# Moving every SBUF tile of a hybrid attention encoder to a multiple of 512 bytes

## The chip, the cores and the metric

The kernel runs on one core of one Trainium2 chip. The metric is the device time of one execution in microseconds (us). The time before is 1574.03 us, the median of three runs (1571.99 to 1578.36).

Five engines work side by side on one core: TensorE (PE in the profile; its weight loads are PEld), VectorE (DVE), ScalarE (ACT), GpSimd (POOL) and SyncE (SP), which here issues the transfers. They share the on-chip memory SBUF, in which a tile is a stretch of bytes at the same address in each of 128 partitions.

## What is computed

One layer of an encoder on 1024 positions of 1024 channels, all in float32, with a conditioning vector c that gives six vectors of shifts, scales and gates:

```
ada = silu(c) @ w_ada + b_ada          # shift1, scale1, gate1, shift2, scale2, gate2
h = rmsnorm(x, g_mix) * (1 + scale1) + shift1
qa, ka, va, qb, kb, vb, ga, gb = split(h @ w_in)
oa = mixture_of_dilations(qa, ka, va)             # three dilated windows, 8 heads of 64
ob = neighbourhood_attention_2d(qb, kb, vb)       # 16 x 64 grid, 8 heads of 64
merged = sigmoid(ga) * (oa @ w_branch_dil) + sigmoid(gb) * (ob @ w_branch_na)
x = x + gate1 * (merged @ w_out)
h2 = rmsnorm(x, g_ffn) * (1 + scale2) + shift2
u = depthwise_conv3(h2 @ w_up)                    # 2 x 2816 channels
x = x + gate2 * ((gelu(u_gate) * u_val) @ w_down)
return rmsnorm(x, g_final)
```

## The kernel before

**Arithmetic.** TensorE multiplies in a float32 form of less precision, so each operand is split into a high and a low part (`split`, line 54: ScalarE copies, then GpSimd or VectorE subtracts) and each product is three matmuls: high by high, high by low, low by high. `product` (line 72) does so for the plain products, on lines 77 to 79; `products` (line 800) does it on lines 822 to 824 for the up and down projections, which are run as a seven-product block scheme. Nearly all of these matmuls load 128x128 weights and stream 512 columns.

**Stages in order of time** (us from the start of the span):

- to about 150: the modulation vectors and the two value projections. The matmuls of `v_products` have h as weights and the tiles a0, a1, b1, b2 as moving operand.
- to about 700: per head pair, the query and key projections (`qk_tiles`), the two attentions, and the gate projections (`gate_tile`) between them. `q_half`, `k_half` and `gate_tile` use weights from the tiles whi and wlo; for the second attention the query product is line 378, with 256 columns each.
- to about 803: the two branch projections with weights from whi and wlo, moving operands o0 and o1.
- to about 886: the output projection (`out_tile`), again with whi and wlo, moving operands mhi and mlo.
- to about 1320: the up projection, 22 blocks of seven products of twelve matmuls. Products "11" and "12" take their weights from whi and wlo, the others from wsh, wsl and big.
- to the end: the down projection, twelve jobs of seven products of nine matmuls, with the same division of the weights, and the last norm.

A planner orders the instructions of each engine, except in stretches that are put under `manual_schedule`. It also makes a tile wait for the last user of the bytes that it takes over (`reuse_waits="tile"`).

**Where tiles lie.** Pools are stacked in SBUF from the low end (left) or, with `side="right"`, from the high end. At address 0 lies a scratch area for transfers that GpSimd issues, 16384 bytes before the change, then four built-in constants of 32 bytes each. So the pool `const` begins at 16512, and everything on the left stands on what lies below it. On the right the stack begins at 229344, which is 32 bytes short of a multiple of 512. Worked out from the sizes in the code, the tiles start at:

| tiles | bytes past a multiple of 512 | side |
|---|---|---|
| idt, sm | 128 | left |
| cs, ones, ada, am1, am2 (32 to 192 bytes each) | 96, 128, 160, 352, 384 | left |
| wraw, whi, wlo (pool `w`) | 416 | left |
| rs (32 bytes, two buffers) | 416, 448 | left |
| all big tiles after pool `w`: t0, a0, a1, b1, b2, qs, ks, kl, vv, P, th, tl, o0, o1, g, wc, big, wsh, wsl, B11 to T4 of the down stage | 480 | left |
| vraw, mt (pool `early`, above the 32 bytes of sig) | 0 | left |
| h, x, gs, mhi, mlo, x2, T1, T2, T3 | 480 | right |

In the down projection the left stack ends exactly where the right one begins (147424).

Lines that the change touches: 41 to 50 (the constants), 93 (rs in `rstd_of`), 256 (sig), 1225 (release of the pools) and 1323 (size of the scratch area).

Of the kernel before, what the change touches and what calls it, by code (L numbers as in the profile page):

```python
# [9 lines left out]
FT = mybir.dt.float32  # L10
# [8 lines left out]
KT = 8  # L19
# [9 lines left out]
def hybrid_encoder(tc, xT, c, w_ada, small, w_in, w_v, p1_bias, p23_bias, na_bias, ln2_mult, ident, w_br, w_out,  # L29
                   w_up, w_down, out):  # L30
    nc = tc.nc
    act, dve, pool, pe, sp = nc.scalar, nc.vector, nc.gpsimd, nc.tensor, nc.sync

    const = tc.alloc_tile_pool(name="const", bufs=1)
    wpool = tc.alloc_tile_pool(name="w", bufs=2)
    dram = tc.alloc_tile_pool(name="scr", bufs=1, space=DRAM)

    def f(ap):
        return ap.bitcast(FT)

    idt = const.tile([128, 128], FT, name="idt")
    sp.dma_start(idt, ident)
    sm = const.tile([128, 248], FT, name="sm")
    cs = const.tile([128, KT], FT, name="cs")
    sp.dma_start(cs, c)
    ones = const.tile([128, 1], FT, name="ones")
    dve.memset(ones, 1.0)
    ada = const.tile([128, 48], FT, name="ada")
    am1 = const.tile([128, KT], FT, name="am1")
    am2 = const.tile([128, KT], FT, name="am2")  # L50
    b_ada, g_mix, g_ffn, g_fin = sm[:, 0:48], sm[:, 48:56], sm[:, 56:64], sm[:, 64:72]
    conv = sm[:, 72:248].rearrange("p (j m) -> p j m", j=4)

# [36 lines left out]
                      stop=last and t == n - 1, skip_group_check=True)  # L90

    def rstd_of(pcol, n):
        r = wpool.tile([128, KT], FT, name="rs", bufs=2)
        dve.tensor_scalar(r[:, :n], pcol[:, :n], 1.0 / D, EPS, OP.mult, OP.add)
        act.activation(r[:, :n], r[:, :n], AF.Sqrt)
        dve.reciprocal(r[:, :n], r[:, :n])
        return r
# [24 lines left out]
    early = tc.alloc_tile_pool(name="early", bufs=1, reuse_waits="tile")  # L122
    ps = tc.alloc_tile_pool(name="ps0", bufs=1, space=PSUM, reuse_waits="tile")
# [129 lines left out]
        for j, t0 in ((0, 0), (8, 240)):  # L253
            sp.dma_start(va_b[j, 0:64, cc].rearrange("(r p) n -> r p n", r=4), v4[:, t0:t0 + 16])

    sig = early.tile([128, KT], FT, name="sig")
    act.activation(sig, cs, AF.Sigmoid)
    dve.tensor_tensor(cs, cs, sig, OP.mult)
    pas = {}
    with tc.manual_schedule(engines={e.engine for e in (sp, act, dve, pool, pe)}):  # L260
# [15 lines left out]
        pcol = norm_sums(accs)  # L276
        acc = ada_rows(rows[0], range(3))
        r = rstd_of(pcol, 4)
        warm(3)
        pb = bcast(r, ps, "pc")  # L280
# [22 lines left out]
        rows = {4: ada_load(4, "t0"), 5: ada_load(5, None)}  # L303
        pcol = norm_sums(accs)
        r = rstd_of(pcol, 4)
        for kp in range(2):
            v_split(raws[kp], vw[1], kp)
# [407 lines left out]
    ps = tc.alloc_tile_pool(name="ps", bufs=1, space=PSUM, reuse_waits="tile")  # L715
    mxpool = tc.alloc_tile_pool(name="mx", bufs=1, side="right", reuse_waits="tile")
# [24 lines left out]
    with tc.tile_pool(name="gate", bufs=1, reuse_waits="tile") as work:  # L741
# [3 lines left out]
        for m in range(KT):  # L745
# [3 lines left out]
            for hf in range(2):  # L749
                sg = []  # L750
                for br in range(2):
# [3 lines left out]
                    p = ps.tile([128, 512], FT, name="pj", bufs=6)  # L755
# [96 lines left out]
    keep = tc.alloc_tile_pool(name="keep", bufs=1, reuse_waits="tile")  # L852
# [128 lines left out]
    add_sums(pcol, sqa, True, False)  # L981
    add_sums(pcol, sq, False, True)
    bc = bcast(rstd_of(pcol, 4), ps, "pbc")
    for k in range(KT):
        dve.tensor_tensor(m1[k], m1[k], bc, OP.mult)
# [23 lines left out]
    with tc.tile_pool(name="up", bufs=2, reuse_waits="tile") as work:  # L1009
# [96 lines left out]
        for t in range(FF):  # L1106
# [8 lines left out]
            for j in gens[t] if t < 2 else up_products(t, sts[t]):  # L1115
# [7 lines left out]
                if t == FF - 1 and j == 3:  # L1123
                    oppool2.release()
                    work2 = tc.alloc_tile_pool(name="down2", bufs=1, side="right", reuse_waits="tile")
# [12 lines left out]
    work1 = {n: tc.alloc_tile_pool(name=n, bufs=1, reuse_waits="tile") for n in ("wsh", "wsl", "B21", "B22", "T4")}  # L1138
# [46 lines left out]
    with tc.manual_schedule(engines={dve.engine}):  # L1185
        for hf, cs in ((0, slice(0, 512)), (1, slice(0, 256)), (1, slice(256, 512))):
            n = cs.stop - cs.start
            late = []
            for m in range(KT):
                if hf == 0 and m + 2 < KT:  # L1190
                    end_w[m + 2] = end_weights(m + 2)
                p = ps.tile([128, 512], FT, name="pj", bufs=6)[:, :n]
# [21 lines left out]
        hf, cs, bc = before  # L1214
# [7 lines left out]
                pool.tensor_tensor(yy, xx, bc, OP.mult)  # L1222
        for m in (0,2,4,6):
            (act if m == 2 else sp).dma_start(out[m:m + 2, :, halves[hf]][:, :, cs].rearrange("t p s -> p t s"), y[m])
    for p in (work2, mxpool, *list(work1.values())[::-1], keep, ps, dram, wpool, const):
        p.release()


# [105 lines left out]
```

## Time and profile before

| | us |
|---|---|
| median of the runs shown | 1574.03 |
| the profiled execution, whole time | 1569.62 |
| its span, first to last instruction | 1567.6 |
| matmuls in the span | 7582 |

The profile is a record of one execution. A group of instructions has its line in the code, engine, tiles (output, then inputs), count, and busy time with the mean of one, or the shortest, median and longest in nanoseconds (ns). Matmuls overlap each other, so the duration of one (389 ns) is longer than the distance from one start to the next; distances are read from the starts in the timeline. Digits are left out of the names of tiles in some views: b1 and b2 are b.

### The profile page before, as it was taken

How to read it: one execution, taken by the hardware profiler on the slowest of the kernel's cores; microseconds unless marked ns; L12 is line 12 of the kernel's file. 1: busy time of each engine (PE TensorE's matmuls, PEld its weight loads, DVE VectorE, ACT ScalarE, POOL GpSimd, SP SyncE). 2: the span in 40 equal slices, each digit the busy share in tenths (PEclk: the TensorE clock that was granted, in tenths of full speed). 3: DMA queues.
4: the chain of work that ended last, by engine and by line, in shares of the span. 5: the costliest groups of instructions: out<-in, count | busy, mean ns of one | idle time of the engine just before them, and what ended most of it. 6: DMA issues, size and time to landing. Idle time of an engine off the chain costs nothing.

```text
span 1567.6 us, 21162 instructions
## 1 busy us (share of the span) xinstructions
PE 1505.0 (96%) x7582; PEld 1266.6 (81%) x7582; DVE 1030.4 (66%) x1873; ACT 777.7 (50%) x1419; POOL 748.4 (48%) x475
## 2 busy tenths in 40 slices
PE   7898999999999999999999989999999999999998
PEld 7687788888878998888778767888888887778787
DVE  7694356576757655525534898677777776877765
ACT  3420566665756666643344444444444446575542
POOL 2310423333214444311146859766677665778621
PEclk8999999999999999999999989999999999999999
DMA  9577632324234565545544212222222223623313
GB/s 378 191 289 268 169 84 89 100 77 114 74 92 133 162 155 134 182 149 183 182 144 148 95 54 94 95 83 88 86 81 81 82 74 135 208 88 126 109 55 108
DMA packets 110000, 205.20 MB, mean 131 GB/s; under 512 B 40356, under 2 KB 55588, under 8 KB 109860
## 3 DMA queue, kind: packets, MB, share of 16 engines
q1 hardware_dynamic: 109624, 203.59, 40.5%
q8 instruction: 60, 0.98, 0.3%
q14 instruction: 44, 0.36, 0.1%
q10 hardware_dynamic: 272, 0.26, 0.1%
HBM read 158.73 MB, written 42.47 MB: 128 GB/s over the span
## 4 chain that ended last, share of the span: by engine, by line
PE 63%; DVE 12%; DMA 9%; POOL 6%; ACT 4%; issue 4%; SPq 1%; DVEq 0%; ACTq 0%; POOLq 0%
PE pj L822 8%; PE pj L823 8%; PE pj L824 8%; PE pj L79 8%; PE pj L77 8%; PE pj L78 8%; DMA wraw<-w_down 3%; DMA g<-gs 2%; DVE mt L151 2%; PE pj L378 2%; PE O L672 2%; POOL wlo L56 2%; POOL wsl L56 2%; DVE big L1017 1%; PE T L660 1%
## 5 line engine op out<-in xcount | busy, mean ns | idle before, releaser
L56 POOL TENSOR_TENSOR wlo<-wraw,whi 128x1024 fp32r<-128x1024 f32 (+1 forms) x77 | 179.4, 2331 | 268.6 <-ACT whi L55 262.3
L77 PE MATMUL pj<-h,whi 128*128 128x512 f32 x448 | 179.7, 401 | 1.8 <-DVE qs L369 1.8
L79 PE MATMUL pj<-h,wlo 128*128 128x512 f32 x448 | 179.9, 402 | 1.3 <-POOL wlo L56 1.3
L78 PE MATMUL pj<-h,whi 128*128 128x512 f32 x448 | 179.3, 400 | 0.0
L1017 DVE SCALAR_TENSOR_TENSOR big<-pj,sm,big 128x512 f32<-128x512 f32 (+2 forms) x252 | 128.4, 565 | 33.1 <-ACT big L1011 33.1
L56 POOL TENSOR_TENSOR wsl<-big,wsh 128x1024 fp32r<-128x1024 f32 (+1 forms) x45 | 109.8, 2442 | 56.9 <-ACT wsh L55 55.7
L1011 ACT ACTIVATE big<-pj,sm 128x512 f32<-128x512 f32 x84 | 63.1, 776 | 123.6 <-DVE pj L840 55.6
L55 ACT ACTIVATE whi<-wraw 128x1024 fp32r<-128x1024 f32 (+1 forms) x79 | 80.7, 1021 | 84.3 <-PE pj L78 27.5
L79 PEld LDWEIGHTS pj<-h,wlo 128*128 128x128 f32 x448 | 85.1, 190 | 16.5 <-POOL wlo L56 1.8
L77 PEld LDWEIGHTS pj<-h,whi 128*128 128x128 f32 x448 | 85.2, 190 | 16.2 <-issue 2.2
L78 PEld LDWEIGHTS pj<-h,whi 128*128 128x128 f32 x448 | 85.1, 190 | 14.6
L449 POOL TENSOR_TENSOR vv<-vv 96x256 fp32r<-96x256 f32 (+2 forms) x32 | 41.1, 1294 | 105.2 <-ACT vv L448 101.8
L498 ACT ACTIVATE P<-P,st 128x256 f32<-128x256 f32 x128 | 64.3, 503 | 51.1 <-DVE st L497 50.8
L385 POOL TENSOR_SCALAR qb<-qs 128x256 fp32r<-128x256 f32 x32 | 26.4, 849 | 122.0 <-PE S L544 57.9
L497 DVE CUSTOM_DVE_ANT_0 P<-S,bias 128x256 f32<-128x256 f32 x128 | 52.4, 420 | 43.4 <-PE S L544 24.7
L650 POOL TENSOR_SCALAR P<-P,stb 128x288 f32<-128x288 f32 (+1 forms) x32 | 40.0, 1249 | 65.6 <-DVE stb L647 58.7
L55 ACT ACTIVATE wsh<-big 128x1024 fp32r<-128x1024 f32 (+1 forms) x45 | 44.9, 1001 | 43.2 <-POOL big L787 21.5
L1044 DVE TENSOR_TENSOR big<-big 128x1024 f32<-128x1024 f32 x22 | 49.7, 2259 | 23.6 <-ACT big L1043 23.6
L56 POOL TENSOR_TENSOR wsl<-wraw,wsh 128x768 fp32r<-128x768 f32 (+1 forms) x23 | 54.5, 2371 | 12.8 <-ACT wsh L55 12.8
L503 DVE TENSOR_TENSOR tl<-T,th 128x512 fp32r<-128x512 f32 x64 | 43.7, 688 | 25.5 <-ACT th L502 25.0
L795 DVE TENSOR_TENSOR wraw<-wraw,big 128x384 f32<-128x384 f32 (+1 forms) x23 | 35.3, 1537 | 34.7 <-POOL big L787 26.5
L79 PE MATMUL pj<-mhi,wlo 128*128 128x512 f32 x128 | 50.7, 396 | 1.8 <-POOL wlo L56 1.8
(366 smaller groups left out, 4785.1 us busy)
## 6 DMA issues: line engine op xcount, KB each, us to landing
wraw<-w_in SPq DMA_DIRECT2D x32, 512.0 KB, 4.4
t<-w_ada SPq DMA_DIRECT2D x24, 512.0 KB, 7.8
big<-w_up SPq DMA_DIRECT2D x22, 512.0 KB, 5.5
wraw<-w_up SPq DMA_DIRECT2D x22, 512.0 KB, 3.5
as<-big SPq DMA_DIRECT2D x22, 512.0 KB, 2.8
big<-as SPq DMA_DIRECT2D x22, 512.0 KB, 6.0
wraw<-w_down SPq DMA_DIRECT2D x24, 384.0 KB, 3.6
x<-w_ada SPq DMA_DIRECT2D x16, 512.0 KB, 8.9
```

Source lines behind the costliest of these rows:

```text
L55: act.activation(hi, raw, AF.Copy)
L56: lo_eng.tensor_tensor(lo, raw, f(hi), OP.subtract)
L77: pe.matmul(psum, whi[:, k0 + k], mhi, start=k == 0, stop=False)
L78: pe.matmul(psum, whi[:, k0 + k], mlo, start=False, stop=False)
L79: pe.matmul(psum, wlo[:, k0 + k], mhi, start=False, stop=k == n - 1)
L497: dve.tensor_tensor_reduce(pp, d, bias, -1.0, BIG, OP.add, OP.min, mi)
L498: act.activation(pp, pp, AF.Exp, bias=mi, scale=-1.0, accum_out=li)
L822: pe.matmul(psum, whi[:, k], bhi, start=j < 4 and k == 0, stop=False, skip_group_check=True)
L823: pe.matmul(psum, whi[:, k], blo, start=False, stop=False, skip_group_check=True)
L824: pe.matmul(psum, wlo[:, k], bhi, start=False, stop=k == n - 1, skip_group_check=True)
L1011: act.activation(y[:, halves[hf]], src, AF.Identity, bias=conv[:, 3, t:t + 1], scale=conv[:, 1, t:t + 1])
L1017: dve.scalar_tensor_tensor(y[:, dst], src, wt, y[:, dst], OP.mult, OP.add)
```

## The change

The constants that are written during the kernel (cs, ones, sig, am1, am2) become slices of one tile `cols` of 384 bytes, sm is padded to 1024 bytes, rs to 256 bytes in each of two buffers. `ada` goes to a pool of its own at the right end and takes 480 bytes there. The scratch area shrinks from 16384 to 8192 bytes.

By the same arithmetic as above: 8192 + 128 + 384 + 512 + 1024 = 10240, so pool `w` begins at 20 x 512, its end is 35328 = 69 x 512, and the right stack begins at 229344 - 480 = 228864 = 447 x 512. All big tiles start at multiples of 512. Tiles of pool `w` go down by 8096 bytes, later ones on the left by 7648, vraw and mt by 7680, and those on the right by 480. Between the two stacks of the down stage 7168 bytes stay free. No instruction is added or removed.

```diff
+    cpool = tc.alloc_tile_pool(name="consts", bufs=1, side="right")
+    ada = cpool.tile([128, 120], FT, name="ada")[:, :48]
+    cols = const.tile([128, 96], FT, name="cols")
+    cs, ones, sig = cols[:, 0:8], cols[:, 8:9], cols[:, 16:24]
+    am1, am2 = cols[:, 24:32], cols[:, 32:40]
     idt = const.tile([128, 128], FT, name="idt")
     sp.dma_start(idt, ident)
-    sm = const.tile([128, 248], FT, name="sm")
-    cs = const.tile([128, KT], FT, name="cs")
+    sm = const.tile([128, 256], FT, name="sm")[:, :248]
     sp.dma_start(cs, c)
-    ones = const.tile([128, 1], FT, name="ones")
     dve.memset(ones, 1.0)
-    ada = const.tile([128, 48], FT, name="ada")
-    am1 = const.tile([128, KT], FT, name="am1")
-    am2 = const.tile([128, KT], FT, name="am2")
...
-        r = wpool.tile([128, KT], FT, name="rs", bufs=2)
+        r = wpool.tile([128, 64], FT, name="rs", bufs=2)
...
-    sig = early.tile([128, KT], FT, name="sig")
...
-    for p in (work2, mxpool, *list(work1.values())[::-1], keep, ps, dram, wpool, const):
+    for p in (work2, mxpool, *list(work1.values())[::-1], keep, ps, dram, wpool, cpool, const):
...
-    nc = bacc.Bacc("TRN2", target_bir_lowering=False, num_devices=1)
+    nc = bacc.Bacc("TRN2", target_bir_lowering=False, num_devices=1, dynamic_dma_scratch_size=8192)
```

## The prediction

> **What bounds the kernel now.** I read the head of the page first, then the chain that ended last, then the table by stages.
>
> ```profile
> PE 1505.0 (96%) x7582; PEld 1266.6 (81%) x7582; DVE 1030.4 (66%) x1873; ACT 777.7 (50%) x1419; POOL 748.4 (48%) x475
> ...
> q1 hardware_dynamic: 109624, 203.59, 40.5%
> ...
> PE 63%; DVE 12%; DMA 9%; POOL 6%; ACT 4%; issue 4%; SPq 1%; DVEq 0%; ACTq 0%; POOLq 0%
> ```
>
> ```profile
> core 0: us, PE busy (x) PEld busy (x) DVE busy (x) ACT busy (x) POOL busy (x), PEclk, DMA share, GB/s
> ...
> 150.00:400.00 250.00, 241.84 (x1387) 208.33 (x1386) 150.22 (x433) 146.68 (x349) 89.03 (x65) 0.99 0.38 105
> 400.00:700.00 300.00, 294.56 (x1818) 262.63 (x1818) 174.50 (x450) 183.33 (x407) 109.87 (x79) 0.99 0.49 134
> 700.00:803.00 103.00, 97.30 (x411) 77.59 (x410) 58.84 (x69) 40.93 (x64) 21.16 (x9) 0.98 0.55 181
> 803.00:886.00 83.00, 82.70 (x376) 68.07 (x375) 37.23 (x41) 37.85 (x53) 53.99 (x29) 1.00 0.44 146
> 886.00:1320.00 434.00, 423.84 (x1849) 347.43 (x1848) 322.56 (x442) 196.07 (x251) 304.35 (x163) 0.99 0.25 84
> ```
>
> TensorE has an instruction in hand for 94 to nearly 100% of these stages, at a granted clock of 0.98 to 1.00. All waits together leave it idle for 1567.6 - 1505.0 = 63 us. So a change of addresses, which removes no instruction, can act in three ways only: an engine takes another time for the same instruction, a transfer takes another time, or a wait or the order changes. For each I look for tiles that lie differently already, since pool `early` (mt, vraw) stands at a multiple of 512 while all others are 416 or 480 past one.
>
> **The change part by part: ScalarE, GpSimd, VectorE, weight loads.** From the views by line, with operations of one shape on tiles of both kinds (shortest, median and longest in ns):
>
> ```profile
> L55 ACT ACTIVATE b<-wraw x4: 613/614/614, 62.0 to 63.6; 128x512 fp32r<-128x512 f32 x4
> L55 ACT ACTIVATE b<-vraw x4: 638/642/643, 66.0 to 67.6; 128x512 fp32r<-128x512 f32 x4
> ```
>
> ```profile
> L56 POOL TENSOR_TENSOR b<-vraw,b x4: 1275/1293/1302, 67.7 to 71.4; 128x512 fp32r<-128x512 f32 x4
> ...
> L56 POOL TENSOR_TENSOR b<-wraw,b x4: 1273/1282/1283, 62.7 to 66.4; 128x512 fp32r<-128x512 f32 x4
> ```
>
> ```profile
> L183 DVE TENSOR_TENSOR mt<-mt x12: 684/692/693, 6.5 to 59.4; 128x512 f32<-128x512 f32 x12
> ```
>
> ```profile
> L759 DVE TENSOR_TENSOR g<-g x16: 691/692/1982, 707.0 to 796.7; 128x512 f32<-128x512 f32 x16
> ```
>
> ```profile
> L140 PEld LDWEIGHTS st<-ones,mt x96: 185/192/339, 18.8 to 146.9; 128*128 128x128 f32 x96
> ...
> L140 PEld LDWEIGHTS st<-cs,t x16: 187/192/193, 46.2 to 48.0; 128*128 128x128 f32 x16
> ```
>
> Reading from vraw at offset 0 instead of wraw at 416 costs ScalarE 28 ns more and GpSimd 11 ns more; an add with all three operands at 0 takes the same 692 ns as with all at 480; a weight load from 0 takes the same 192 ns as from 480. I cost these engines at **nothing**. Bounds: 28 ns more on some 250 splits, about as many as line 55 has, is 7 us of ScalarE work, of which 4% (its share of the chain) would count, so 0 to +0.3 us.
>
> **TensorE.** Here two offsets can be told apart. The timeline of one up block has three products in a row, weights from whi and wlo (416) in the first, from wsh and wsl (480) in the second; the third ends the second:
>
> ```profile
> 1003.39 0.39 PE L822 MATMUL pj<-B21hi,whi 128*128 128x512 f32 x1
> ...
> 1006.14 0.39 PE L822 MATMUL pj<-T1hi,wsh 128*128 128x512 f32 x1
> ...
> 1008.86 0.39 PE L822 MATMUL pj<-T3hi,wsh 128*128 128x512 f32 x1
> ```
>
> Twelve matmuls take 2.75 us with the weights of pool `w` and 2.72 us with the others: 229.2 against 226.7 ns, 2.5 ns apart. The groups of lines show it elsewhere, with matmuls of the same shape and no idle time before them:
>
> ```profile
> L78 PE MATMUL pj<-mlo,whi 128*128 128x512 f32 x21 | 8.3, 394 | 0.0
> L77 PE MATMUL pj<-mhi,whi 128*128 128x512 f32 x21 | 8.2, 392 | 0.0
> L79 PE MATMUL pj<-mhi,wlo 128*128 128x512 f32 x21 | 8.2, 388 | 0.0
> ```
>
> ```profile
> L823 PE MATMUL pj<-B11lo,whi 128*128 128x512 f32 x4 | 1.6, 394 | 0.0
> ...
> L823 PE MATMUL pj<-T1lo,wsh 128*128 128x512 f32 x4 | 1.6, 390 | 0.0
> ```
>
> The mean of 394, 392 and 388 is 391.3, which is 2.3 above the 389 of most groups of the up stage. What sets the tiles of pool `w` apart by their address is that their weights lie 64 bytes off the phase of the moving operand (416 against 480), where wsh, wsl, big and h as weights lie in phase with theirs. After the change all are in phase, at 0. That wlo shows no surplus of its own speaks against a plain rule of offsets; I take the triple as the unit, since its three matmuls push each other.
>
> How many: by the loops, 448 x 3 = 1344 in the query, key and gate products, 384 in the branches, 384 in the output projection, 22 x 24 = 528 in the up and 12 x 18 = 216 in the down projection: 2856 matmuls by 2.5 ns is **7.1 us of TensorE time**. Between 63% (its share of the chain) and 98% (its busy share in these stages) of it reaches the end; I take 80%, so **-5.7 us**. When TensorE is quicker there, the next in line are the splits on GpSimd (6% of the chain), which is why not all is kept. Bounds of the phase effect: from -7 us, when all is kept, to nothing.
>
> For the rest of a matmul's cost I can only ask whether the start of the moving operand counts. In the second attention, the keys of grid column 0 start at 480 past a multiple of 512 (32 past one of 64), and those of column 3 are 160 bytes on, at 128 (a multiple of 64 and of 128). Both stream 288 columns:
>
> ```profile
> 568.63 0.29 PE L639 MATMUL S<-ks,qs 128*128 128x288 f32 x1
> ...
> 569.16 0.28 PE L672 MATMUL O<-th,vv 96*128 96x256 f32 x1
> ```
>
> ```profile
> 628.78 0.30 PE L639 MATMUL S<-ks,qs 128*128 128x288 f32 x1
> ...
> 629.31 0.49 PE L660 MATMUL T<-idt,P 128*96 128x128 f32 x3
> ```
>
> Four matmuls take 0.53 us in both. So a better aligned start alone buys nothing that these rows show. The Trainium skill's page "SBUF — State Buffer" (section "Specifications (TRN2)") gives cachelines of 16 bytes as what an access pays for; since every tile before starts at a multiple of 32, by that rule nothing at all would change. The equal 0.53 us agrees, the 2.5 ns of pool `w` doesn't.
>
> **Transfers.** The issues view has transfers out of and into both kinds of tile:
>
> ```profile
> t<-w_ada SPq DMA_DIRECT2D x24, 512.0 KB, 7.8
> ...
> wraw<-w_up SPq DMA_DIRECT2D x22, 512.0 KB, 3.5
> ...
> gs<-gs SPq DMA_DIRECT2D x32, 256.0 KB, 2.6
> ...
> vraw<-w_v SPq DMA_DIRECT2D x4, 512.0 KB, 6.3
> vas<-mt SPq DMA_DIRECT2D x8, 256.0 KB, 8.3
> ```
>
> Into vraw (offset 0) 512 KB take 6.3 us and into t (480) 7.8 us, both in the crowded first stage; out of mt (0) half as much takes 8.3 us, out of gs (480) 2.6 us in a quieter one. The signs disagree, so I take **0**, and keep the bound for a rival. All issues are SP's and ACT's, none GpSimd's, so the smaller scratch area costs nothing.
>
> **Waits and order.** A left tile now lies 7168 bytes lower against a right one, which changes who waits for whom in three places. The right-hand mhi no longer lies over u1 of the attention; the transfer that last read it and the first write of mhi are far apart. The third buffer of wsh no longer lies over mhi, but all buffers of wsl do still reach over it or already did, and mhi's last reader is done before wsh is first written. Tiles th and tl lie over less of x, which the value projections of the stage before have done with.
>
> ```profile
> 690.60 2.59 DMA ob<-u
> ```
>
> ```profile
> L79 PE MATMUL pj<-mhi,wlo x128: 388/388/628, 789.3 to 884.5; 128*128 128x512 f32 x128
> L55 ACT ACTIVATE mhi<-g x16: 612/615/629, 708.6 to 798.8; 128x512 fp32r<-128x512 f32 x16
> ```
>
> ```profile
> L55 ACT ACTIVATE wsh<-big x45: 830/1061/1064, 886.5 to 1485.2; 128x1024 fp32r<-128x1024 f32 x33, 128x768 fp32r<-128x768 f32 x12
> ```
>
> Nothing there is late now, so **0**. That cols is one tile could make a write of am1 wait for TensorE's readers of cs and ones; VectorE already waits there for the sums that these readers make. The chain in order of time has one such sum:
>
> ```profile
> 18.77 1.07 PE st L140 x8
> ```
>
> If the cover failed, such a wait would come four times: 4 x 1.07 = +4 us.
>
> **Sum.** 0 - 5.7 + 0 + 0. The profiled execution took 1569.62 us and would take 1563.9. It lies below all three runs shown, so I set the sum against their median: 1574.0 - 5.7 = **1568.3 us**. A measurement of this kernel tells 0.5% from no change, 7.9 us: the bounds are 1566.1 and 1581.9.
>
> **Rivals.**
> 1. *The change does nothing for time*: the 2.5 ns belong to something else about pool `w` (its place in memory, or its buffers being written beside). For it: wlo at 416 shows no surplus. 1574.0.
> 2. *The fixed part of a matmul shrinks.* From 226.7 ns for 512 columns and 132.5 ns for 288, a column costs 0.4205 ns and 11.4 ns don't depend on the columns. If misalignment is their cause, 5196 matmuls of 512 columns by 11.4 ns by 80% is 47 us: 1527, or 1550 if half goes. Against it: the equal 0.53 us. The Trainium skill ("TensorE: Matmul & The Clock Gate", section "Back-to-back issue gap") has N/2.4 + 2.5 ns, an estimated 215.8 for 512 columns, 10.9 below this trace, which would put the time at about 1529.
> 3. *Transfers get shorter.* A transfer of 512 KB holds each of 16 engines for 0.405 x 1567.6 x 0.524 / 203.59 = 1.63 us of its 3.5. If one part in nine of that goes, it is 0.11 x 0.47 of the chain's 141 us of DMA, 7.3 us: with the forecast 1561. The Trainium skill ("DMA: Bandwidth & Descriptors", section "How a descriptor splits into AXI transactions") says that a descriptor which doesn't start at a multiple of 256 bytes fetches bytes it doesn't use, one transaction more than eight for 2048 bytes. The rows above don't bear it out.
> 4. *Slower: offset 0 is worse than 480 for the stream of matmuls*, as 416 is. No row has both operands at 0. By the same 2.5 ns on the 5196 - 2856 that are at 480 now and none gained on the rest: 5.9 us; at 5 ns on all 5196, by 80%, 21 us: 1580 to 1595, middle 1586. It decides from 1.9 ns on all.
> 5. *The planner puts another order*, since tiles wait for others: -10 to +15 us, in the attention stages, which aren't under a hand-written order.
>
> **How the numbers follow.** Forecast 0.36 (1562 to 1574; a third of it below 1566.1), rival 1 0.20, rival 2 0.10, rival 3 0.08, rival 4 0.14, rival 5 0.12 (faster 0.04, same 0.02, slower 0.06). Faster: 0.12 + 0.10 + 0.08 + 0.04 = 0.34; same: 0.24 + 0.20 + 0.02 = 0.46; slower: 0.14 + 0.06 = 0.20. The range leaves out most of rival 2 below 1553 and the upper half of rival 4 above 1586.
>
> **What would show it.** Right: twelve matmuls with whi and wlo take 2.72 us, as those with wsh; splits, adds and landings unchanged. Rival 2: twelve take under 2.70 us everywhere. Rival 4: over 2.75 everywhere. Rival 5: an engine's instructions in another sequence in the attention stages. The forecast is wrong if the 2.75 us stays, or if 2.72 moves at all.

## The result, and the profile after

The changed kernel took 1561.43 us (median of four runs, 1559.17 to 1565.12) beside 1573.75 us for the kernel before on the same chip: a ratio of 0.992, with a 95% interval of 0.9891 to 0.9948. That is 12.3 us less, where 5.7 us less had been forecast; measured again in e5 below it was 0.9935 (0.9912 to 0.9957). The profiled execution has a span of 1559.6 us and took 1561.49 us in all.

The head of the page after, the rows that answer to those of before:

```profile
PE 1498.4 (96%) x7582; PEld 1264.8 (81%) x7582; DVE 1031.4 (66%) x1873; ACT 778.1 (50%) x1419; POOL 747.2 (48%) x475
...
q1 hardware_dynamic: 109624, 203.59, 40.0%
...
PE 65%; DVE 12%; DMA 8%; POOL 6%; issue 4%; ACT 4%; SPq 1%; DVEq 0%; ACTq 0%; POOLq 0%
```

TensorE is busy for 6.6 us less (1505.0 to 1498.4), the other engines for the same time within 2 us. The transfers move the same 203.59 MB and hold their engines for 40.0% of a shorter span instead of 40.5%. So two things have become shorter: matmuls and transfers.

**The matmuls.** The timeline of an up block after the change, first matmul of each of the three products (line 822 of before is line 821 here):

```profile
996.88 0.39 PE L821 MATMUL pj<-B21hi,whi 128*128 128x512 f32 x1
...
999.60 0.39 PE L821 MATMUL pj<-T1hi,wsh 128*128 128x512 f32 x1
...
1002.32 0.39 PE L821 MATMUL pj<-T3hi,wsh 128*128 128x512 f32 x1
```

Twelve matmuls now take 2.72 us with the weights whi and wlo, as they do with wsh; before it was 2.75. The groups by line and shape, of the stages from 700 to 1320 us, before and then after (mean of one in ns behind the comma):

```profile
L78 PE MATMUL pj<-mlo,whi 128*128 128x512 f32 x128 | 51.4, 402 | 0.2 <-DVE mlo L56 0.2
...
L823 PE MATMUL pj<-B11lo,whi 128*128 128x512 f32 x88 | 34.7, 394 | 0.0
...
L823 PE MATMUL pj<-T1lo,wsh 128*128 128x512 f32 x88 | 34.4, 391 | 0.2 <-DVE T1lo L769 0.2
```

```profile
L78 PE MATMUL pj<-mlo,whi 128*128 128x512 f32 x128 | 50.6, 396 | 0.2 <-DVE mlo L56 0.2
...
L822 PE MATMUL pj<-T1lo,wsh 128*128 128x512 f32 x88 | 34.3, 390 | 0.3 <-DVE T1lo L768 0.3
L822 PE MATMUL pj<-B11lo,whi 128*128 128x512 f32 x88 | 34.3, 389 | 0.0
```

The surplus of the groups with whi is gone: 402 to 396 ns, 394 to 389, while the group with wsh stays (391, 390).

**The other engines.** ScalarE's splits and VectorE's adds, after:

```profile
L55 ACT ACTIVATE b<-wraw x4: 613/614/615, 62.1 to 63.6; 128x512 fp32r<-128x512 f32 x4
L55 ACT ACTIVATE b<-vraw x4: 640/643/646, 66.1 to 67.6; 128x512 fp32r<-128x512 f32 x4
```

```profile
L183 DVE TENSOR_TENSOR mt<-mt x12: 683/693/694, 6.8 to 59.5; 128x512 f32<-128x512 f32 x12
```

Both sources and the outputs now lie at multiples of 512, and the split from vraw still takes 29 ns more than the one from wraw. So the 28 ns that the prediction read there were never a matter of the place within 512 bytes.

**The transfers.** The issues view (last number: median us from issue to landing), first the rows of after that answer to those of before, then a tile that the prediction did not look at, vv, the values of one head, before and after:

```profile
wraw<-w_up SPq DMA_DIRECT2D x22, 512.0 KB, 3.5
...
gs<-gs SPq DMA_DIRECT2D x32, 256.0 KB, 2.5
...
vas<-mt SPq DMA_DIRECT2D x8, 256.0 KB, 8.4
```

```profile
vv<-vas SPq DMA_DIRECT2D x8, 256.0 KB, 4.3
...
vv<-vab SPq DMA_DIRECT2D x8, 224.0 KB, 4.8
```

```profile
vv<-vas SPq DMA_DIRECT2D x8, 256.0 KB, 3.9
...
vv<-vab SPq DMA_DIRECT2D x8, 224.0 KB, 4.3
```

The large transfers land as before. Those into vv land half a microsecond earlier. They consist of pieces of 256 bytes, one for each row of 64 values, each landing 256 bytes into a slot of 512. ScalarE waits for them; the waits view (total us, times, longest), before and after:

```profile
ACT vv L448 <- DMA vv<-vb: 21.9, 9, 5.9
...
ACT vv L448 <- DMA vv<-vab: 12.9, 6, 6.0
```

```profile
ACT vv L447 <- DMA vv<-vb: 17.8, 9, 4.2
...
ACT vv L447 <- DMA vv<-vab: 10.5, 5, 4.7
```

**A trap.** Set the two traces beside each other, matmul by matmul, and the largest single gain lies between 426 and 464 us: 3.8 us. In the chain of before in order of time stands

```profile
432.95 7.63 DMA vv<-vb
```

and behind this wait one stretch of 3.4 us in which TensorE runs at half its clock (windows view of before; the clock is the third number from the end):

```profile
443.60:447.00 3.40, 3.40 (x13) 2.91 (x12) 2.98 (x11) 1.27 (x5) 1.42 (x2) 0.50 0.00 0
```

It is tempting to put this down to the shorter pieces. But the same matmuls are 2.8 us earlier against that trace in e1, where no large tile changes its place within 512 bytes, and 2.6 us in e2. The wait is a feature of that one profiled execution. TensorE even had other matmuls to run through most of it, and stood idle only from 440.59 to 442.52 us (timeline of before):

```profile
442.52 0.38 PE L527 MATMUL O<-th,vv 128*128 128x256 f32 x1 [1.93 <-ACT th L502]
```

The Trainium skill ("TensorE: Matmul & The Clock Gate", Part 1) says that the clock is halved after a window of some 3.4 us without work. The 0.50 and the length of 3.4 us agree with it; the idle time doesn't, since 1.93 us came before the half clock here.

### The profile page after: what moved, and what is told of

It reads as the page before. It is cut to its first block, busy times and chain, and to the rows that moved or that the text cites. A ratio compares the mean times of both kernels' runs of the same rounds, so it can differ in the third digit from the quotient of the medians.

```text
span 1559.6 us, 21161 instructions
## 1 busy us (share of the span) xinstructions
PE 1498.4 (96%) x7582; PEld 1264.8 (81%) x7582; DVE 1031.4 (66%) x1873; ACT 778.1 (50%) x1419; POOL 747.2 (48%) x475
## 3 DMA queue, kind: packets, MB, share of 16 engines
q1 hardware_dynamic: 109624, 203.59, 40.0%
## 4 chain that ended last, share of the span: by engine, by line
PE 65%; DVE 12%; DMA 8%; POOL 6%; issue 4%; ACT 4%; SPq 1%; DVEq 0%; ACTq 0%; POOLq 0%
PE pj L822 9%; PE pj L821 9%; PE pj L823 9%; PE pj L79 8%; PE pj L78 8%; PE pj L77 8%; DMA g<-gs 2%; DVE mt L151 2%; PE pj L377 2%; PE O L671 2%; DMA wraw<-w_down 2%; POOL wlo L56 2%; POOL wsl L56 2%; DVE big L1016 1%; PE T L659 1%
```

## The experiments

Theory at the start: the gain has two parts, matmuls whose weights and moving operand now agree in phase, and transfers whose pieces now start at multiples of 256 bytes. Rivals: the scratch area or the lower addresses as such; the phase alone (the forecast); the transfers alone. In all kernels every engine executes the same sequence of instructions as before.

Three measures from the records of each trace go with the times. *Three matmuls*: median time from the start of a high-by-high matmul to the start of the next, over the products of the up and down stages with whi; where the times spread, their range. *Surplus*: all distances below 245 ns from the start of a 512-column matmul to the start of the matmul behind it, each less 226.7 ns, summed. *Packets*: mean of those of 256 bytes; share of those of 2048 bytes that take the shortest usual time (84 ns or less); time of all packets divided by the 16 engines. "Both right" below means weights and moving operand at the same place modulo 256, and packets at multiples of 256.

| kernel | tiles, past a multiple of 512 | three matmuls, ns | surplus, us | 256 B, ns | 2048 B short | all, us | ratio to before (95%) |
|---|---|---|---|---|---|---|---|
| before | 480, pool w 416 | 687 | 8.9 | 22.1 | 68% | 640.8 | 1 |
| after | 0 | 680 | 4.7 | 19.0 | 93% | 630.3 | 0.9920 (0.9891 to 0.9948) |
| e1 | as before | 687 | 8.8 | 21.9 | 69% | 638.7 | 1.0004 (0.9988 to 1.0021) |
| e2 | 480 | 680 | 4.7 | 22.2 | 68% | 641.5 | 0.9996 (0.9979 to 1.0012) |
| e10 | 480, once more | 680 | 4.7 | 21.9 | 67% | 642.0 | 0.9998 (0.9985 to 1.0012) |
| e3 | left 0, right 480 | 680 to 702 | 25.8 | 18.9 | 70% | 632.6 | 1.0055 (1.0035 to 1.0074) |
| e4 | 0, pool w 448 | 687 | 8.9 | 18.8 | 92% | 629.3 | 0.9977 (0.9963 to 0.9991) |
| e9 | 0, pool w 128 | 690 to 706 | 18.7 | 19.0 | 92% | 631.5 | 1.0023 (1.0008 to 1.0037) |
| e8 | 0, pool w 256 | 680 | 5.0 | 18.8 | 93% | 627.8 | 0.9945 (0.9922 to 0.9968) |
| e5 | 0, the change again | 680 | 4.9 | 18.9 | 93% | 628.9 | 0.9935 (0.9912 to 0.9957) |
| e6 | 64 | 680 | 4.9 | 21.7 | 80% | 635.6 | 0.9972 (0.9958 to 0.9986) |
| e7 | 256 | 680 | 5.0 | 18.9 | 93% | 631.8 | 0.9951 (0.9934 to 0.9968) |
| e11 | 0, vv 64 | 680 | 5.1 | 21.7 | 93% | 633.2 | 0.9966 (0.9951 to 0.9981) |
| e12 | 64, vv 0 | 680 | 4.9 | 18.8 | 81% | 632.6 | 0.9974 (0.9956 to 0.9991) |

Each ratio is taken to runs of the kernel before on the same chip (median 1570.53 to 1573.75 us in the five sets). 0.001 is 1.6 us.

**The scratch area alone.** Against before:

```diff
-    nc = bacc.Bacc("TRN2", target_bir_lowering=False, num_devices=1)
+    nc = bacc.Bacc("TRN2", target_bir_lowering=False, num_devices=1, dynamic_dma_scratch_size=8192)
```

> The kernel before with the scratch area of 8192 bytes alone: left tiles go down by 8192 bytes, every offset past a multiple of 512 stays (weights of pool w at 416, the rest at 480). Offset theory (the offset of the weights in 512 bytes sets the pace): twelve matmuls with whi and wlo still take 2.75 us, with wsh 2.72; time of before within 0.3%, 1569 to 1578. Place theory (what counts is where in memory the tiles lie, or which right-hand tiles they cover): the 2.75 us becomes 2.72 and the time falls by some 0.5 to 0.8%, to about 1562.

1.0004, and the matmuls and the packets keep their pace. Moving everything on the left down by 8192 bytes is worth nothing: the gain is not in the scratch area, nor in lower addresses.

**The phase alone: all large tiles at 480.** Against before, with the scratch area of e1:

```diff
+    sig = const.tile([128, KT], FT, name="sig")
+    const.tile([128, KT], FT, name="pad")
...
-        r = wpool.tile([128, KT], FT, name="rs", bufs=2)
+        r = wpool.tile([128, 64], FT, name="rs", bufs=2)
...
-    sig = early.tile([128, KT], FT, name="sig")
```

> The kernel before with a scratch area of 8192 bytes, constants padded by 64 bytes and rs padded: every big tile lies 480 bytes past a multiple of 512, left and right, none at a multiple. Phase theory (weights and moving operand must start at the same offset): the same gain as the change, triples of matmuls with whi and wlo at 680 ns instead of 687, time within 0.3% of the changed kernel, about 1562. Alignment theory (the start at a multiple of 512, or of 64, counts): triples with whi and wlo keep 687 ns or change otherwise, time nearer to before, 1569 or more.

> The kernel of e2 once more: all large tiles at 480. e2 gave 0.9996 with its matmuls at 680 ns and its 256-byte pieces at 22 ns; e6, with all at 64, has the same two and gave 0.9972. Theory A (the two are the same kernel in all that counts, and e2 and e6 were the two sides of one spread): 0.997 to 0.999. Theory B (480 costs something that 64 does not): 0.9995 to 1.001 again.

The matmuls do what the forecast says, 680 ns for three and a surplus of 4.7 us as after the change. The time doesn't, against about 1562 us that the phase theory expected of e2: 0.9996 and 0.9998 (1570.19 and 1570.98 us). The transfers are as long as before; the issues view of e2:

```profile
vv<-vas SPq DMA_DIRECT2D x8, 256.0 KB, 4.5
...
vv<-vab SPq DMA_DIRECT2D x8, 224.0 KB, 5.0
```

So the phase alone, in a kernel whose transfers stay at 480, buys nothing that can be measured. Theory B of e10 holds.

Where it was given back can be counted in part, one profile each. From TensorE's busy time I take off half of what falls into stretches at half clock, as lost to the clock. That leaves 1505.0 - 21.5 = 1483.5 us of work before and, reckoned alike, 1482.9 in e1, 1480.5 in e2, 1478.3 in e10 and 1478.7 after the change. So e2 and e10 save 3.0 and 5.2 us of work, the change 4.8. But TensorE is idle for 65.4 and 65.8 us, more than in any of the other twelve profiles (57.7 to 63.6; 62.5 before, 61.3 after the change). The time lost to the clock tells nothing here: it is 26.9 us in e1, more than in e2 or e10. Which wait carries the added idle time of some 3 us isn't singled out.

**The weights' offset, with aligned transfers.** Against after, pool w alone is moved (e4; e9 and e8 likewise, with 32 and 64 elements of padding and rs of 48 and 32):

```diff
+    const.tile([128, 112], FT, name="pad")
...
-        r = wpool.tile([128, 64], FT, name="rs", bufs=2)
+        r = wpool.tile([128, 8], FT, name="rs", bufs=2)
```

and in e3 ada goes back to the left, so that all tiles on the right are 32 bytes off those on the left:

```diff
-    cpool = tc.alloc_tile_pool(name="consts", bufs=1, side="right")
-    ada = cpool.tile([128, 120], FT, name="ada")[:, :48]
+    ada = const.tile([128, 128], FT, name="ada")[:, :48]
```

> The changed kernel with pool w 64 bytes short of a multiple of 512 (offset 448), all else at multiples of 512. Phase theory: triples with whi and wlo return to 687 ns, as 64 bytes is the distance of before; the time loses the 2856 x 2.4 ns x 80% = 5.5 us, to about 1567. Alignment theory with a grain of 64 bytes: 448 is a multiple of 64, so 680 ns stays and the time is that of the changed kernel, about 1561; with a grain of 512: 687 or more.

> The changed kernel with pool w alone 256 bytes past a multiple of 512. If weights and moving operand must agree in 512 bytes, triples with whi and wlo get 684 to 702 ns, as 32 and 64 bytes gave (699, 687), and the time rises by 0.3 to 0.6%. If they must agree in 256 bytes or less, 680 and no change of time. Below 680 would mean that the distance can be chosen for a gain.

> The changed kernel with only pool w (wraw, whi, wlo) moved to 128 past a multiple of 512; everything else at 0. Run e4 had it 64 bytes below (448): three matmuls with whi 687 ns, ratio 0.9977; run e8 at 256: 680 ns, 0.9945. Theory A (weights and moving operand must agree modulo 128): 680 ns, ratio 0.994 as e8. Theory B (they must agree modulo 256): 687 ns, ratio 0.998 as e4. Theory C (the surplus grows with the distance in bytes): over 687 ns and a ratio over 0.998. Pieces of 256 bytes stay at a mean of 19 ns in all three, since vv does not move.

> The changed kernel with ada back on the left (padded to 512 bytes): left tiles at multiples of 512, right ones (h, mhi, mlo, x2, T1, T2, T3) at 480. Phase theory: products whose weights and moving operand lie on different sides get the surplus (whi with h, wsh with T1, T2, T3 in the up stage, 7 ns on a triple of 680), those with both on the left (whi with B11, B21, o0, o1) stay at 680; some 3400 matmuls by 2.3 ns by 80% is 6 us above the changed kernel, about 1568. Alignment of the weights alone: all triples with whi, wlo, wsh, wsl at 680, time as the changed kernel, 1562.

Timelines of the same up block in e4, e9 and e3:

```profile
1002.74 0.39 PE L822 MATMUL pj<-B21hi,whi 128*128 128x512 f32 x1
...
1005.49 0.39 PE L822 MATMUL pj<-T1hi,wsh 128*128 128x512 f32 x1
...
1008.21 0.39 PE L822 MATMUL pj<-T3hi,wsh 128*128 128x512 f32 x1
```

```profile
986.37 0.40 PE L822 MATMUL pj<-B21hi,whi 128*128 128x512 f32 x1
...
989.17 0.40 PE L822 MATMUL pj<-T1hi,wsh 128*128 128x512 f32 x1
...
991.92 0.39 PE L822 MATMUL pj<-T3hi,wsh 128*128 128x512 f32 x1
```

```profile
991.41 0.39 PE L820 MATMUL pj<-B21hi,whi 128*128 128x512 f32 x1
...
994.16 0.40 PE L820 MATMUL pj<-T1hi,wsh 128*128 128x512 f32 x1
...
996.96 0.40 PE L820 MATMUL pj<-T3hi,wsh 128*128 128x512 f32 x1
```

At 448, 64 bytes below the moving operand, the 2.75 us of before are back, while wsh keeps 2.72. At 128 they are 2.80. In e3 it is the product T1 with wsh, right against left, that takes 2.80. At 256 (e8) three matmuls are back at 680 ns. So what counts, at the distances tried here, is whether weights and moving operand start at the same place modulo 256, and with which difference: none 680 ns, 64 bytes 687, 128 bytes 690 to 706, 32 bytes 698 to 702. A common offset (0, 64, 256 or 480) costs a matmul nothing. For e9 theory C comes nearest, but the surplus does not simply grow with the distance: 32 bytes cost about as much as 128.

The expectation of e3 missed two things. A product whose operands differ by 32 bytes pays some 19 ns on three matmuls, not 7, so the kernel took 1579.71 us where about 1568 had been expected. And products whose two operands agree don't all stay at 680 ns when the product ahead of them is off by 32 or 128 bytes: B21 with whi in e3 takes 2.75 us, and so does T1 with wsh in e9. Behind products that are 64 bytes off (before, e4) the twelve of T1 take 2.72. Why the surplus carries over isn't known.

The times follow, with transfers alike in e4, e8 and e9: 0.9945 at 680 ns, 0.9977 at 687, 1.0023 at 690 to 706. From the mean of the four kernels that have both right (after, e5, e7, e8: 0.9938) to e9 are 13.4 us for 18.7 - 4.9 = 13.8 us more surplus, to e4 6.1 us for 4.0, where the interval of e4 alone is 2.2 us to each side. Here the pace of the matmuls passes to the end nearly in full. e3 is not as clean, since its tiles on the right have unaligned transfers.

**The common offset.** Against after, all tiles at 64 (e6; e7 likewise with 64 and 56 elements, at 256), beside the change itself (e5):

```diff
-    ada = cpool.tile([128, 120], FT, name="ada")[:, :48]
+    ada = cpool.tile([128, 104], FT, name="ada")[:, :48]
...
+    const.tile([128, 16], FT, name="pad")
```

> The changed kernel itself, on the chip of this set. Two-part theory (equal offsets of weights and moving operand, which e2 has and e4 lacks; and 256-byte pieces of the vv loads that start at a multiple of 256, which e4 has and e2 lacks): the sum of e4's gain of 0.23% and of the 2856 x 2.4 ns x 80% = 5.5 us that e4 gives away, 0.35%: ratio 0.994. Matmul pace alone: as e2, 0.9996. First measurement was right as it stood: 0.992.

> The changed kernel with every big tile 64 bytes past a multiple of 512, left and right: equal offsets, starts at multiples of 64, not of 256. Both theories of the matmul pace say triples of 680 ns. If 256-byte pieces are slowed by crossing a multiple of 256, they are again longer than 18 ns in a third of the cases (mean 22) and the time is that of e2, 0.9996 of before, some 0.4% above the changed kernel. If they only have to start at a multiple of 64, their mean stays at 19 and the time is that of the changed kernel.

> The changed kernel with every big tile 256 bytes past a multiple of 512. Grain of 256 or 64 bytes: as the changed kernel within 0.2%, pieces of 256 bytes at a mean of 19 ns, triples at 680. Grain of 512 bytes: pieces at 22 ns, time nearer to before.

256 does as well as 0: packets at 18.9 ns, 0.9951 against 0.9935, intervals overlapping. 64 doesn't: 21.7 ns, 0.9972. With the matmuls at 680 ns in all of them, the time follows the transfers: 0.9997 at 480 (mean of e2 and e10, packets 641.8 us in all), 0.9972 at 64 (635.6), 0.9938 with both right (629.7 on average). From end to end 9.3 us of time go with 12.1 us of packets.

The Trainium skill ("DMA: Bandwidth & Descriptors", "How a descriptor splits into AXI transactions") says that a descriptor which starts off a multiple of 256 bytes also fetches the bytes from the boundary below its start. For a piece of 256 bytes that makes an estimated 10 beats of 32 bytes instead of 8 at 64, and 15 at 224, where the pieces of a tile at 480 land. That carries the rule, which speaks of fetching, over to the side that writes, since it is the end of these transfers in vv that moved. The order of the measured means agrees (18.9, 21.7, 22.1 ns), the size doesn't: most packets keep their 18 ns at any offset, and only the share above grows, from about 10% to 30% and 34%.

**Which transfers.** Against after, vv alone at 64 (e11), and against e6 vv alone back at a multiple of 512 (e12, with 112 in place of 16):

```diff
-        vv = sm_pool.tile([128, 16, 128], FR, name="vv")
+        vv = sm_pool.tile([128, 2176], FR, name="vv")[:, 16:2064].rearrange("p (c n) -> p c n", c=16)
```

> The changed kernel with only the tile vv (the attention's values) moved to 64 past a multiple of 512, so that its 256-byte pieces land 64 past a multiple of 256; all other tiles stay at 0. Its weights are then 64 bytes off the moving operand th, a price p of 0 to 2 us that e12 has too. Theory A (the gain of the transfers comes from the pieces into vv): pieces at 22 ns, the waits of ScalarE for vv back to 20 us or more, ratio about 0.997 as e6 (all at 64) or above by p. Theory B (it comes from the larger transfers, whose packets are shorter as well): pieces at 22 ns, but ratio 0.994 to 0.995 plus p.

> The kernel of e6 (all tiles at 64 past a multiple of 512) with only vv moved to a multiple of 512, so that its 256-byte pieces lie on multiples of 256 and the larger transfers don't. Its weights are 64 bytes off th as in e11, price p. Theory A (the pieces into vv carry it): pieces at 19 ns, ratio 0.994 to 0.995 plus p. Theory B (the larger transfers carry it): pieces at 19 ns, ratio 0.997 as e6 plus p. Half the difference between what e11 loses on the change and what e12 gains on e6 is the worth of the pieces, since p falls out.

The pieces follow vv, 21.7 and 18.8 ns, and so do ScalarE's waits for them (both rows together 34.8 us before, 28.3 after, 31.3 in e11, 28.9 in e12). But the times don't separate the theories. e11 loses 0.0031 on e5, as theory A says; e12 gains nothing on e6 (0.9974 against 0.9972), as theory B says. A price p that both have cancels when loss and gain are added, not when they are subtracted as the expectation has it: the pieces are worth (0.0031 - 0.0002) / 2 = 0.0015 or 2.3 us, with an uncertainty as large as itself. The price p of a weight 64 bytes off is not seen in these matmuls of 256 columns: a median of 119 ns from start to start in e11 and e12, 120 after.

The packet times by size leave both theories standing too. Of the 10.5 us that the change takes off all packets, those of 256 bytes have 6.0. From 480 (e2, e10) to 64 (e6), 5.3 of 6.1 us are larger packets, and the time falls by 0.0025; from 64 to the four kernels with both right, 5.3 of 5.9 us are pieces of 256 bytes, and it falls by 0.0034. Which transfers carry the gain stays open.

## Why the prediction was right in mechanism and short in size

**The number.** 1561.43 us lies within the prediction's range (1553 to 1586), just outside the forecast's own band (1562 to 1574).

**What bounds the kernel: right.** TensorE's pace passes to the end (e4, e9), and the three ways that were named were the right ones to look at; two of them act.

**TensorE, -5.7 us: the mechanism is right, the terms are not all.** The surplus of pool w was a matter of phase between weights and moving operand, on the strength of 2.75 against 2.72 us, and it went. The 16-byte cachelines of the Trainium skill ("SBUF — State Buffer", "Specifications (TRN2)"), by which nothing would change, do not cover 680 to 706 ns for three matmuls at starts that are all multiples of 32. The surplus fell by 8.9 - 4.7 = 4.2 us, not 7.1, so the term was too large: of the 2856 matmuls, the 1344 of the query, key and gate products keep an uneven pace of about 229.5 ns (some four in ten groups of three take 690 to 700 ns) after the change too; why isn't known. "I take 80%" was worth testing: alone the phase gave about nothing (e2, e10), on top of aligned transfers 6.1 us (0.9977 to 0.9938). What is kept is no constant of the kernel; it changes with the offset of the transfers' tiles, by which wait isn't shown. The prediction named splits on GpSimd as the next in line: TensorE's wait for wlo is 7.7 us on average in the nine kernels whose operands agree and 6.6 in the five others, about 1 us of what isn't kept.

**Transfers, "The signs disagree, so I take 0": the step that failed.** Alone they are worth 0.0023 or 3.6 us (e4 against before, 1.4 to 5.8), and they decide whether the phase pays. The rows compared were landings of large transfers in crowded stages, whose packets gain under 2% each (2048 bytes 95.9 to 94.2 ns, 4096 bytes 191.9 to 190.4, where 256 bytes go from 22.1 to 19.0); no row of vv, with 30720 of the 109624 packets, was looked at. All the pieces into vv lay at one offset before, so no row of theirs could have told the effect. That is a reason for a bound, not for 0. Rival 3 had the bound, 7.3 us, and the rule, and was given 0.08 because "the rows above don't bear it out". What came is the forecast and rival 3 together, in kind. That rival put both at 1561, and this agreement is luck: it is made of 5.7 and 7.3 us, where the runs show 0.5 and 3.6 us for each part alone and 5.6 us that need both.

**Engines at nothing, order at nothing, the scratch area at nothing: right.** Splits and adds are unchanged, every engine's sequence is the same (rival 5 falls), e1 is 1.0004. Waits weren't quite nothing: ScalarE's for vv fell by 6.5 us, with the transfers.

**The others.** Rival 1: the surplus of whi follows its offset, not its place (e4, e8, e9). Rival 2: twelve matmuls take 2.72 us, no less. Rival 4: streams at 0 are as quick as at 480, 680 ns for three.

**Sum.** Transfers alone -3.6 us, phase alone -0.5 us (e2 and e10, not told from 0), both -9.7 us (mean of after, e5, e7 and e8; the first measurement said -12.3). The two parts don't add up: 5.6 of the 9.7 us need both, with an uncertainty of some 3 us from the intervals. Matmuls and transfers are shown as the two causes; the wait by which each needs the other is not.

## What to carry to other kernels

In a kernel that TensorE bounds, let the weights and the moving operand of a matmul start at the same place modulo 256 bytes, and let tiles that transfers fill with small pieces start at multiples of 256; padding of a few hundred bytes in the constants does both for every tile stacked above, as long as the tiles between have sizes that are multiples of 256. Test such a change with both parts in place: the faster matmuls alone gave nothing here. When a trace holds no instance of the new offset, keep a bound for it, and don't take 0 because other rows disagree.

## What had not been expected of the hardware

- A matmul of 128x128 weights and 512 columns has a pace that depends on the offset between its two operands: 680 ns for three with none (modulo 256), 687 at 64 bytes, 690 to 706 at 128, 698 to 702 at 32; at 32 and 128 part of it carries over to the product behind.
- Packets of 256 bytes took 18.9 ns on average at multiples of 256 and 21.7 to 22.2 elsewhere, by a longer tail, not by a longer typical packet.
